# Gate and up projections as Strassen's seven products in three of four feed-forward blocks, with weight sums and residual updates by accumulating DMA

## The chip, the cores and the metric

One core of a Trainium2 chip runs the whole kernel. The metric is the device time of one execution in microseconds. TensorE multiplies, VectorE, ScalarE and Pool (GpSimd) do the elementwise work, SP and Pool issue the DMAs; each engine works through its own instructions in order.

## The reference

Two layers of a transformer block on a latent stream of 512 tokens (A) and a context stream of 256 tokens (C), both 1024 wide. Each layer is a feed-forward block (FFN), four token mixers in parallel with an output projection, and a second FFN. What the change touches is the FFN:

```python
def pre_norm(h, g, shift, scale):
    return rms_norm(h, g) * (1.0 + scale) + shift

def swiglu(h, wg, wu, wd):
    return (jax.nn.silu(h @ wg) * (h @ wu)) @ wd

x = x + 0.5 * mx[2] * swiglu(pre_norm(x, norm1_g[i], mx[0], mx[1]), ffn1_wg[i], ffn1_wu[i], ffn1_wd[i])
```

The hidden width is 2816, that is 22 blocks of 128. `mx` and `mc` are nine modulation vectors per layer, a 1024 x 9216 product of the conditioning vector. In the second layer only stream A is needed after the mixers, so of the four FFNs three run on both streams (768 tokens) and the last on A alone. All of it is in fp32.

## The kernel before

Activations stand transposed, channels on partitions and tokens along the free axis. An fp32 product is made of three matmuls (`mm3`, L286 to L288): every operand is split into a rounded high part and the rest, and high x high, high x low and low x high are added up in PSUM. The normed input is kept as such a pair, `xnh` and `xnl`, for A and for C.

`ffn` runs over the 22 hidden blocks in groups of 6, 6, 5 and 5. For a block, `weight` loads a 128 x 1024 tile for the gate and one for the up projection (`wr`, on SP's queue), ScalarE rounds it to `wh` (L265) and VectorE subtracts to get `wl` (L270). Per tile there are 8 contraction steps of three matmuls for C (256 columns) and for A (512 columns, or two halves A0 and A1 in the first `NS` blocks). ScalarE applies SiLU (L322), VectorE multiplies (L323), and the result is split into `hh` and `hl`. After a group, its down projection runs over 8 output chunks, and VectorE adds each result, times the gate `modG`, to the residual `x` (L344).

The last group's down projection goes in three passes (C, A0, A1), each with its own loads of the down weights. Within it the sum of squares of the new residual is gathered (`sumsq`: square on ScalarE, sum on Pool, or on VectorE for the end of A1), and `norm` (L256 to L260: two operations on VectorE and one on ScalarE per chunk, after a row statistic `nsum`, `rb` that passes TensorE, VectorE and Pool) makes the next stage's input for one part while the next part is still being projected.

The modulation vectors (`ada`, L157 and L160) are computed beside the FFNs: Pool loads 128 x 1024 tiles, `AB` buffers deep, and VectorE reduces each against one or two vectors; `fill` hands them out at an even rate. 128 tiles and 224 reductions are spread over the three two-stream FFNs. PSUM has eight banks in three rings, `p` (4), `r` (2) and `d` (2).

The order of instructions within each engine's queue is not that of the program text: a planner orders them ahead of time by its own estimate of durations, with the program's order as priority; buffers are given out in that order too.

## Time and profile before

| | us |
|---|---|
| median of three runs | 3222.77 |
| lowest, highest | 3219.68, 3239.86 |
| the profiled execution: time | 3218.36 |
| the profiled execution: span from first to last instruction | 3216.6 |

The profile is one execution. Busy time counts an engine's instructions; matmuls overlap in the array, so TensorE's busy share is not its share of the peak. In a timeline a row's duration can reach into the next row's start, so the distance between starts is the pace. The first FFN lies at 46 to 606 us, the second at about 1226 to 1762, the third at 1762 to 2320 and the last at 2838 to 3206.

### The profile page before, as it was taken

The page shows a single profiled execution, that of the slowest core. Times are in us where ns is not written, and L with a number is a line of the kernel's source. Part 1 is how long each engine was busy: PE and PEld are TensorE (multiplying, and loading weights), DVE is VectorE, ACT ScalarE, POOL GpSimd, SP SyncE. Part 2 cuts the span into 40 slices and gives each one's busy share as a digit, 9 for nine tenths or more (in the row PEclk, how much of TensorE's full clock was granted, in tenths as well). Part 3 has the DMA queues.
Part 4 walks back from the last instruction along what each step waited for, and adds up shares of the span by engine and source line. Part 5 has one row for each costly group of instructions (what it writes and reads, how often), then busy time and mean ns, then how long its engine had stood idle before and what let it go on. Part 6 is the DMA issues. An engine that isn't in the chain of part 4 may idle for free.

```text
span 3216.6 us, 48071 instructions
## 1 busy us (share of the span) xinstructions
PE 3092.6 (96%) x19394; PEld 2699.5 (84%) x19394; DVE 1670.6 (52%) x2964; ACT 1061.2 (33%) x1912; POOL 391.3 (12%) x646
## 2 busy tenths in 40 slices
PE   7999999998999999999999999999997899999998
PEld 4888888886788888888889988888885788788887
DVE  4994232736855449994236332323646745353334
ACT  3212112545444433121224212122455353342223
POOL 1110000410233011120002000000311332000001
PEclk9999999998999999999999999999998999899999
DMA  6662221514543335683124221212523523323333
GB/s 246 200 204 59 70 68 48 176 56 125 153 98 89 85 127 180 202 264 120 53 73 125 61 64 60 73 53 68 149 74 121 149 73 83 122 87 99 96 99 105
DMA packets 133485, 358.42 MB, mean 111 GB/s; under 512 B 17968, under 2 KB 31792, under 8 KB 132880
## 3 DMA queue, kind: packets, MB, share of 16 engines
q1 hardware_dynamic: 101200, 256.52, 26.0%
q0 software_dynamic: 32064, 98.85, 10.9%
q8 instruction: 152, 2.49, 0.3%
q14 instruction: 69, 0.57, 0.1%
HBM read 317.94 MB, written 39.65 MB: 111 GB/s over the span
## 4 chain that ended last, share of the span: by engine, by line
PE 55%; DVE 3%; DMA 1%; ACT 1%; issue 1%; POOL 0%; SPq 0%; POOLq 0%; DVEq 0%; ACTq 0%
PE dacc L286 4%; PE dacc L287 4%; PE dacc L288 4%; PE uA L288 4%; PE uA L286 4%; PE uA L287 4%; PE gA L287 4%; PE gA L286 4%; PE gA L288 4%; PE guC L288 3%; PE guC L286 3%; PE guC L287 3%; PE o L738 2%; PE pj L286 1%; PE pj L288 1%; PE pj L287 1%
## 5 line engine op out<-in xcount | busy, mean ns | idle before, releaser
L265 ACT CAST wh<-wr 128x1024 fp32r<-128x1024 f32 (+5 forms) x443 | 394.8, 893 | 1262.9 <-PE dacc L287 452.8
L270 DVE TENSOR_TENSOR wl<-wr,wh 128x1024 fp32r<-128x1024 f32 (+5 forms) x443 | 459.6, 1040 | 411.3 <-ACT wh L265 391.0
L286 PE MATMUL dacc<-hh,wh 128*128 128x256 f32 (+1 forms) x1392 | 451.3, 326 | 1.7 <-ACT wh L265 1.5
L288 PE MATMUL dacc<-hh,wl 128*128 128x256 f32 (+1 forms) x1392 | 450.7, 326 | 1.4 <-DVE wl L270 1.3
L287 PE MATMUL dacc<-hl,wh 128*128 128x256 f32 (+1 forms) x1392 | 452.1, 326 | 0.0
L286 PE MATMUL guC<-xnhC,wh 128*128 128x256 f32 x1056 | 298.8, 284 | 3.3 <-ACT xnhC L259 1.7
L288 PE MATMUL guC<-xnhC,wl 128*128 128x256 f32 x1056 | 299.4, 284 | 0.9 <-DVE wl L270 0.9
L287 PE MATMUL guC<-xnlC,wh 128*128 128x256 f32 x1056 | 299.0, 283 | 0.0
L160 DVE CUSTOM_DVE_ANT_0 adao<-adaw,silr,adab 128x1024 f32<-128x1024 f32 x224 | 287.1, 1282 | 11.8 <-DMA adaw<-ada_t 8.5
L286 PE MATMUL gA<-xnhA,wh 128*128 128x512 f32 (+1 forms) x752 | 284.2, 379 | 2.0 <-ACT xnhA L259 2.0
L286 PEld LDWEIGHTS dacc<-hh,wh 128*128 128x128 f32 x1392 | 261.4, 188 | 27.7 <-ACT wh L265 2.6
L287 PE MATMUL gA<-xnlA,wh 128*128 128x512 f32 (+1 forms) x752 | 282.9, 378 | 1.0 <-DVE xnlA L260 1.0
L288 PEld LDWEIGHTS dacc<-hh,wl 128*128 128x128 f32 x1392 | 261.2, 188 | 26.9 <-DVE wl L270 2.0
L288 PE MATMUL uA<-xnhA,wl 128*128 128x512 f32 (+1 forms) x752 | 283.0, 376 | 0.6 <-DVE wl L270 0.6
L286 PE MATMUL uA<-xnhA,wh 128*128 128x512 f32 (+1 forms) x752 | 283.1, 376 | 0.4 <-ACT wh L265 0.4
L287 PE MATMUL uA<-xnlA,wh 128*128 128x512 f32 (+1 forms) x752 | 283.1, 376 | 0.0
L288 PE MATMUL gA<-xnhA,wl 128*128 128x512 f32 (+1 forms) x752 | 282.8, 376 | 0.0
L287 PEld LDWEIGHTS dacc<-hl,wh 128*128 128x128 f32 x1392 | 261.4, 188 | 25.0
L344 DVE SCALAR_TENSOR_TENSOR xA<-dacc,modG,xA 128x512 f32<-128x512 f32 (+1 forms) x160 | 102.1, 641 | 253.5 <-PE dacc L288 253.2
L286 PEld LDWEIGHTS guC<-xnhC,wh 128*128 128x128 f32 x1056 | 202.3, 192 | 7.4 <-ACT wh L265 2.4
L287 PEld LDWEIGHTS guC<-xnlC,wh 128*128 128x128 f32 x1056 | 202.9, 192 | 2.7
L288 PEld LDWEIGHTS guC<-xnhC,wl 128*128 128x128 f32 x1056 | 203.0, 192 | 1.9 <-DVE wl L270 1.5
(352 smaller groups left out, 5737.7 us busy)
## 6 DMA issues: line engine op xcount, KB each, us to landing
wr<-wgu SPq DMA_DIRECT2D x176, 512.0 KB, 3.6
adaw<-ada_t POOLq DMA_DIRECT2D x128, 512.0 KB, 4.4
wr<-wd SPq DMA_DIRECT2D x120, 320.0 KB, 3.0
wr<-wd SPq DMA_DIRECT2D x64, 384.0 KB, 3.2
wr<-win SPq DMA_DIRECT2D x44, 512.0 KB, 3.7
adaw<-ada_w SPq DMA_DIRECT2D x32, 256.0 KB, 5.2
hl<-eh SPq DMA_DIRECT2D x32, 192.0 KB, 3.1
hl<-el SPq DMA_DIRECT2D x24, 192.0 KB, 3.4
```

Source lines behind the costliest of these rows:

```text
L160: nc.vector.tensor_tensor_reduce(o, w, self.silr[:, v], 1.0, self.adab[:, l, m:m + 1], ALU.mult, ALU.add, self.mods[l][:, m, v:v + 1])
L265: nc.scalar.copy(hi, src)
L270: (nc.vector if leng == "V" else nc.gpsimd).tensor_tensor(lo, src, hi.bitcast(F32), op=ALU.subtract)
L286: nc.tensor.matmul(out, lhsT=wh, rhs=xh, start=start, stop=False)
L287: nc.tensor.matmul(out, lhsT=wh, rhs=xl, start=False, stop=False)
L288: nc.tensor.matmul(out, lhsT=wl, rhs=xh, start=False, stop=stop)
L344: nc.vector.scalar_tensor_tensor(out=x, in0=acc, scalar=gate[:, i, m, r:r + 1], in1=x, op0=ALU.mult, op1=ALU.add)
L738: nc.tensor.matmul(o[:, q0 + q], lhsT=p[:, q * 128:q * 128 + 128], rhs=v(kb), start=False, stop=kb == 3 and q == n // 128 - 1)
```

## The change

In the three two-stream FFNs `ffn` is replaced by `ffn2`. A block's gate and up weights, over the two halves of the 1024 channels, are a 2 x 2 matrix of 128 x 512 tiles (A11, A12 for the gate, A21, A22 for up), and the normed input is a 2 x 2 matrix (two halves of the channels by two halves of 384 tokens, each 256 of A and 128 of C). Winograd's form of Strassen's scheme gives the four results with seven products of 4 contraction steps instead of eight. `sums7` forms the sums of the inputs once per FFN, after block 0, which is computed in the plain way; the fourth of them takes the place of a quarter of the normed input. `chunk7` makes one block: the weight sums S1 and S3 are made by loading one tile and accumulating another onto it by a DMA that Pool issues, S2 and S4 on VectorE; each of the seven sources is split by `block`. Two blocks overlap, seven slots apart, with their products in turn. The results are added on VectorE as they leave PSUM.

The down projection goes in groups of 3 blocks (the last of 4), one output chunk per slot, three slots after a group's last block. Except in the last group, ScalarE evacuates the result times the gate into `y`, and an accumulating DMA from Pool adds `y` to the residual. Weight buffers hold 512 columns, eight raw ones and five pairs of split ones; the modulation has two buffers instead of four, and its scratch output is shared with `sumsq`. Projections of stream A that permute tokens go in two halves of 256 columns. The last FFN keeps `ffn`, for A alone. The scratch for Pool's DMA descriptors is halved. The core of the diff:

```diff
-AB = 4
-NS, LAG = [0, 2, 2, 2], 2
+AB = 2
+LAG = 2
 NR = "r"
 SSV, SSM = ("A1",), 5
+
+RB, BB, WAIT = 8, 5, 3
 PASSES = {1: [["A0"], ["A1"]], 2: [["C"], ["A0"], ["A1"]]}
+
+GROUPS2 = [(f, f + 3) for f in range(0, 18, 3)] + [(18, 22)]
+SLOTS = 7
...
+        self.XN = {w: [p.tile([128, 4, 2, 384], F32R, name="xn%s%d" % (w, i)) for i in range(2)] for w in "hl"}
...
-                    o = self.wa.tile([128, 1024], F32, tag="wo", name="adao", bufs=1)
+                    o = self.fs.tile([128, TX], F32, tag="sq", name="adao", bufs=1).bitcast(BF16)
...
+        if self.wblk:
+            if w <= 512:
+                raw = self.wp.tile([128, 512], F32, tag="wd", name="wd", bufs=2)
+                self.nc.sync.dma_start(out=raw[:, :w], in_=ap)
+                bs = [self.block(raw[:, :w])]
+            else:
+                bs = []
+                for c in range(0, w, 512):
+                    raw = self.wp.tile([128, 512], F32, tag="wr", name="wr", bufs=RB)[:, :min(w - c, 512)]
+                    self.nc.sync.dma_start(out=raw, in_=ap[:, c:min(w, c + 512)])
+                    bs.append(self.block(raw))
+            return Cols([b[0] for b in bs]), Cols([b[1] for b in bs])
...
+    def block(self, src):
+
+        w = src.shape[-1]
+        hi = self.wp.tile([128, 512], F32R, tag="bh", name="wh", bufs=BB)
+        lo = self.wp.tile([128, 512], F32R, tag="bl", name="wl", bufs=BB)
+        self.split(src, hi[:, :w], lo[:, :w])
+        return hi, lo
...
+    def ffn2(self, l, i, save, then):
+        nc = self.nc
+        fi = 0 if i == 0 else 1
+        up, dn, gate = self.I["wgu"], self.I["wd"], self.modG
+        H = {}
+        def hid(f):
+            H[f] = [self.hp.tile([128, 768], F32R, tag=t, name=t).rearrange("p (h t) -> p h t", h=2) for t in ("hh", "hl")]
+            return H[f]
+        W = [self.weight(up[l, fi, 0, :, j], 1024) for j in range(2)]
+        temps = {kk: [self.hp.tile([128, 768], F32, tag=t, name="x" + t).rearrange("p (k c) -> p k c", k=2)
+                      for t in ("hh", "hh", "hl", "hl")] for kk in (0, 2)}
+        hh, hl = hid(0)
+        for u in self.units(["A", "C"]):
+            gu = self.psum((128, 2, TC), name="gu", ring="p")
+            for j in range(2):
+                wh, wl = W[j]
+                for k in range(KD):
+                    self.mm3(self.two(gu[:, j], u), wh[:, k * 128:(k + 1) * 128], wl[:, k * 128:(k + 1) * 128],
+                             self.xn("h", u, k), self.xn("l", u, k), k == 0, k == KD - 1)
+            sg = self.fs.tile([128, 384], F32, tag="sg", name="sg", bufs=1)[:, :TC]
+            h = self.fs.tile([128, 384], F32, tag="s1", name="h")[:, :TC]
+            nc.scalar.activation(sg, gu[:, 0], ACTF.Silu)
+            nc.vector.tensor_tensor(h, sg, gu[:, 1], op=ALU.mult)
+            self.split(self.two(h, u), self.tok(hh, u), self.tok(hl, u))
+        self.sums7(temps)
+        def down(f0, f1, m, us, last):
+            nf = f1 - f0
+            while (l, 3 * i + 2) not in self.adone:
+                self.sided += 1
+                next(self.side)
+            wh, wl = self.weight(dn[l, fi, m, :, f0:f1].rearrange("p f c -> p (f c)"), nf * 128)
+            for v in us:
+                p, cols, t = self.unit(v)
+                r = 0 if p == "A" else 1
+                acc = self.psum((128, t), name="dacc", ring=None if last else "d")
+                if not last and v == us[0]:
+                    y = self.wp.tile([128, TX + TC], F32, tag="y", name="y", bufs=2)
+                for f in range(f0, f1):
+                    c = slice((f - f0) * 128, (f - f0) * 128 + 128)
+                    self.mm3(self.two(acc, v), wh[:, c], wl[:, c], self.tok(H[f][0], v), self.tok(H[f][1], v), f == f0, f == f1 - 1)
+                if not last:
+                    nc.scalar.activation(y[:, 0:TX] if p == "A" else y[:, TX:], acc, ACTF.Copy, scale=gate[:, i, m, r:r + 1])
+                    continue
+                x = self.X[p][:, m, cols]
+                nc.vector.scalar_tensor_tensor(out=x, in0=acc, scalar=gate[:, i, m, r:r + 1], in1=x,
+                                               op0=ALU.mult, op1=ALU.add)
+                self.sumsq(v, m)
+                if p in save:
+                    nc.gpsimd.dma_start(out=self.xd[p][:, m, cols], in_=x)
+            if not last:
+                nc.gpsimd.dma_start(out=self.X[""][:, m], in_=y, accum_op=ALU.add)
+        order = sorted((SLOTS * (f - 1) + 2 * n, f, n) for f in range(1, NF) for n in range(SLOTS))
+        chunks, tasks, gi = {}, [], 0
+        for t, f, n in order:
+            if n == 0:
+                chunks[f] = self.chunk7(up[l, fi, f], hid, f)
+            next(chunks[f], None)
+            if n == SLOTS - 1 and f == GROUPS2[gi][1] - 1 and f < NF - 1:
+                tasks += [(t + WAIT, *GROUPS2[gi], m) for m in range(KD)]
+                gi += 1
+            if tasks and tasks[0][0] <= t:
+                down(*tasks.pop(0)[1:], ("C", "A"), False)
+            self.fill((t + 1) / (SLOTS * (NF - 1)))
+        for k in tasks:
+            down(*k[1:], ("C", "A"), False)
+        due = []
+        for us in PASSES[2]:
+            for m in range(KD):
+                if due and m >= LAG:
+                    then(due.pop(0))
+                down(*GROUPS2[-1], m, us, True)
+            due += us
+        for u in due:
+            then(u)
+    def sums7(self, temps):
+        nc = self.nc
+        self.T7 = {w: [self.tp7.tile([128, 4, 384], F32R, name="t%s%d" % (w, n)) for n in range(3)] for w in "hl"}
+        for c in (slice(256, 384), slice(0, 256)):
+            for kk in (0, 2):
+                ks = slice(kk, kk + 2)
+                x12, x22, x11, x21 = [t[:, :, c] for t in temps[kk]]
+                for x, i, j, e in ((x12, 0, 1, nc.vector), (x22, 1, 1, nc.vector), (x11, 0, 0, nc.gpsimd), (x21, 1, 0, nc.gpsimd)):
+                    e.tensor_tensor(x, *[self.XN[w][i][:, ks, j, c].bitcast(F32) for w in "hl"], op=ALU.add)
+                minus = dict(scalar=-1.0, op0=ALU.mult, op1=ALU.subtract)
+                nc.vector.tensor_tensor(x11, x11, x12, op=ALU.subtract)
+                nc.vector.tensor_tensor(x12, x22, x12, op=ALU.subtract)
+                nc.vector.scalar_tensor_tensor(out=x22, in0=x11, in1=x22, **minus)
+                nc.vector.scalar_tensor_tensor(out=x21, in0=x22, in1=x21, **minus)
+                for x, n in ((x22, 1), (x11, 0), (x12, 2)):
+                    self.split(x, *[self.T7[w][n][:, ks, c] for w in "hl"])
+                self.split(x21, *[self.XN[w][0][:, ks, 1, c] for w in "hl"])
+    def chunk7(self, ap, hid, f):
+        nc = self.nc
+        def raw(j, h, *more):
+            t = self.wp.tile([128, 512], F32, tag="wr", name="wr", bufs=RB)
+            nc.sync.dma_start(out=t, in_=ap[:, j, 512 * h:512 * h + 512])
+            for j, h in more:
+                nc.gpsimd.dma_start(out=t, in_=ap[:, j, 512 * h:512 * h + 512], accum_op=ALU.add)
+            return t
+        S1 = raw(1, 0, (1, 1))
+        A11 = raw(0, 0)
+        S3 = raw(0, 0, (1, 0))
+        A12 = raw(0, 1)
+        A22 = raw(1, 1)
+        T = lambda n: [self.T7[w][n] for w in "hl"]
+        B = lambda i, j: [self.XN[w][i][:, :, j] for w in "hl"]
+        s = lambda: self.wp.tile([128, 512], F32, tag="ws", name="ws", bufs=2)
+        small = lambda tag: self.fs.tile([128, 384], F32, tag=tag, name=tag, bufs=1 if tag in ("u3", "sg") else 2)
+        def product(bank, src, x, first):
+            wh, wl = self.block(src)
+            for k in range(4):
+                c = slice(k * 128, k * 128 + 128)
+                self.mm3(bank, wh[:, c], wl[:, c], x[0][:, k], x[1][:, k], first and k == 0, k == 3, True)
+        add = lambda e, o, a, b, op=ALU.add: e.tensor_tensor(o, a, b, op=op)
+        a = self.psum((128, 384), name="pa", ring="p")
+        product(a, A11, B(0, 0), True)
+        s1 = small("s1")
+        nc.scalar.copy(s1, a)
+        yield
+        b = self.psum((128, 384), name="pb", ring="p")
+        S2 = s()
+        add(nc.vector, S2, S1, A11)
+        product(b, S2, T(1), True)
+        u2 = small("u2")
+        add(nc.vector, u2, b, s1)
+        yield
+        c = self.psum((128, 384), name="pc", ring="r")
+        product(c, S1, T(0), True)
+        S4 = s()
+        add(nc.vector, S4, A12, S2)
+        yield
+        product(b, S3, T(2), False)
+        u3 = small("u3")
+        add(nc.vector, u3, b, s1)
+        add(nc.vector, u3, c, u3)
+        yield
+        product(a, A12, B(1, 0), False)
+        sg = small("sg")
+        nc.scalar.activation(sg, a, ACTF.Silu)
+        yield
+        product(c, S4, B(1, 1), False)
+        add(nc.vector, u2, c, u2)
+        nc.scalar.activation(u2, u2, ACTF.Silu)
+        hh, hl = hid(f)
+        nc.vector.scalar_tensor_tensor(out=u3, in0=u2, scalar=-1.0, in1=u3, op0=ALU.mult, op1=ALU.mult)
+        self.split(u3, hh[:, 1], hl[:, 1])
+        yield
+        product(b, A22, B(0, 1), False)
+        add(nc.vector, s1, b, s1)
+        nc.vector.scalar_tensor_tensor(out=s1, in0=sg, scalar=-1.0, in1=s1, op0=ALU.mult, op1=ALU.mult)
+        self.split(s1, hh[:, 0], hl[:, 0])
...
-            for u in self.units([p], halves):
+            for u in self.units([p], halves or (perm and p == "A")):
...
-        if l == 1:
-            self.beside([])
-        self.ffn(l, 2, parts, (), then, NS[2 * l + 1])
+        if l == 0:
+            self.ffn2(l, 2, (), then)
+        else:
+            self.ffn(l, 2, then, 2)
...
-    nc = bacc.Bacc("TRN2", target_bir_lowering=False, num_devices=1, dynamic_dma_scratch_size=4096)
+    nc = bacc.Bacc("TRN2", target_bir_lowering=False, num_devices=1, dynamic_dma_scratch_size=2048)
```

## Rows read from the trace of the kernel before

**Rows 1.** The page: busy us (share of the span) and instructions of each engine.

```profile
PE 3092.6 (96%) x19394; PEld 2699.5 (84%) x19394; DVE 1670.6 (52%) x2964; ACT 1061.2 (33%) x1912; POOL 391.3 (12%) x646
```

**Rows 2.** Busy time by stretch: stretch, length, then each engine, granted clock, DMA share, GB/s.

```profile
0.00:46.00 46.00, 24.13 (x84) 6.64 (x84) 11.79 (x26) 15.39 (x24) 7.51 (x13) 1.00 0.93 346
46.00:98.00 52.00, 50.84 (x278) 44.74 (x279) 44.88 (x75) 19.35 (x32) 6.64 (x15) 0.93 0.44 144
98.00:554.00 456.00, 456.00 (x2627) 402.01 (x2626) 233.78 (x353) 92.82 (x136) 19.90 (x37) 1.00 0.35 106
...
1706.00:1764.00 58.00, 57.56 (x438) 55.16 (x437) 42.20 (x76) 32.54 (x61) 19.18 (x20) 1.00 0.51 141
1764.00:1816.00 52.00, 51.48 (x385) 49.30 (x384) 26.54 (x51) 18.32 (x34) 0.71 (x1) 1.00 0.26 82
1816.00:2264.00 448.00, 448.00 (x2585) 395.42 (x2585) 133.81 (x183) 91.60 (x134) 0.00 (x0) 1.00 0.21 62
```

**Rows 3.** TensorE's timeline, third FFN: start, us, line, operation, tiles, shape.

```profile
1815.83 0.28 PE L286 MATMUL guC<-xnhC,wh 128*128 128x256 f32 x1
...
1821.46 0.28 PE L288 MATMUL guC<-xnhC,wl 128*128 128x256 f32 x1
1821.58 0.40 PE L286 MATMUL gA<-xnhA,wh 128*128 128x512 f32 x1
...
1831.81 0.39 PE L286 MATMUL uA<-xnhA,wh 128*128 128x512 f32 x1
```

**Rows 4.** VectorE's timeline around the third seam (same columns; idle time in brackets).

```profile
1701.20 0.69 DVE L323 TENSOR_TENSOR h<-sg,uA 128x512 f32<-128x512 f32 x1 [3.38 <-PE uA L288]
1701.81 0.82 DVE L270 TENSOR_TENSOR wl<-wr,wh 128x640 fp32r<-128x640 f32 x1
...
1762.78 0.47 DVE L344 SCALAR_TENSOR_TENSOR xA<-dacc,modG,xA 128x256 f32<-128x256 f32 x1
1763.17 0.41 DVE L222 TENSOR_TENSOR ssA<-ssA,sq 128x256 f32<-128x256 f32 x1
1763.50 0.47 DVE L260 SCALAR_TENSOR_TENSOR xnlA<-nt,mod,xnhA 128x256 fp32r<-128x256 f32 x1
```

**Rows 5.** Groups by line and form, whole span: count, busy us, mean ns, idle before.

```profile
L160 DVE CUSTOM_DVE_ANT_0 adao<-adaw,silr,adab 128x1024 f32<-128x1024 f32 x224 | 287.1, 1282 | 11.8 <-DMA adaw<-ada_t 8.5
...
L157 POOL DMA_DIRECT2D adaw<-ada_t x128 | 68.4, 535 | 353.6 <-DVE mod L160 328.3 <-DVE modG L189 12.2 <-DVE wl L270 11.1
...
L265 ACT CAST hh<-h 128x512 fp32r<-128x512 f32 x88 | 54.7, 622 | 9.4 <-DVE h L323 7.3
...
L222 POOL TENSOR_TENSOR ssA<-ssA,sq 128x256 f32<-128x256 f32 x48 | 42.0, 875 | 472.0 <-issue 345.9 <-DVE ssA L222 89.1 <-ACT sq L221 36.5
```

**Rows 6.** DMA issues: tiles, queue, count, size, median us to landing.

```profile
wr<-wgu SPq DMA_DIRECT2D x176, 512.0 KB, 3.6
adaw<-ada_t POOLq DMA_DIRECT2D x128, 512.0 KB, 4.4
...
ka<-hl POOLq DMA_DIRECT2D x12, 384.0 KB, 4.5
...
qa<-hl POOLq DMA_DIRECT2D x8, 384.0 KB, 6.9
```

**Rows 7.** Waits of SP's DMA queue: us in total, times, longest.

```profile
SPq L278 <- DVE wl L270: 2125.8, 391, 30.6
```

**Rows 8.** The third seam: the last down matmuls (tile view), TensorE's and VectorE's timeline.

```profile
L288 PE MATMUL dacc<-hh,wl x120: 277/280/362, 1717.8 to 1762.4; 128*128 128x256 f32 x120
...
1776.77 0.59 PE L236 MATMUL rb<-dg,ones 128*128 128x256 f32 x2
...
1784.03 0.88 DVE L260 SCALAR_TENSOR_TENSOR xnlA<-nt,mod,xnhA 128x256 fp32r<-128x256 f32 x2 [0.19 <-ACT xnhA L259]
```

**Rows 9.** TensorE's timeline at the first FFN's start.

```profile
51.24 0.63 PE L287 MATMUL gA<-xnlA,wh 128*128 128x512 f32 x1
51.67 0.63 PE L288 MATMUL gA<-xnhA,wl 128*128 128x512 f32 x1
```

More of the change, by code (lines that the diff above doesn't have):

```diff
@@ L328, in ffn @@
             due = []
-            for us in PASSES[len(parts)] if last else [self.units(parts, False)]:
+            for us in PASSES[1] if last else [["A"]]:
                 for m in range(KD):
@@ L1349, in run @@
         self.ada_prep()
+        self.adone = set()
         for l in range(2):
```

163 lines of the change are left out of this document (89 added, 74 removed).

## The prediction

> **What bounds the kernel now.** I read the busy shares first: TensorE is busy for 96% of the span, VectorE for 52% [rows 1]. A share is an average, so the next view is the busy time by stretch [rows 2]. In 98:554 and 1816:2264, the middle of the first and the third feed-forward block (FFN), TensorE is busy for every microsecond, at full granted clock, with VectorE at 51% and 30% (233.78 of 456, 133.81 of 448). There nothing but matmul time counts. At the seams it is different: in 1706:1764 and 1764:1816, where one FFN ends and the next begins, VectorE has 42.20 of 58 and 26.54 of 52 us and TensorE loses about half a microsecond in each. So time can be gained by fewer matmul columns in the middles, and lost where the seams, or VectorE, become the limit.
>
> The pace of a matmul is its start-to-start distance, not its duration. From the first to the last of 48 matmuls of 256 columns there are 47 steps in 5.63 us, 0.1198 us each; of 512 columns, 45 steps in 10.23 us, 0.2273 us each [rows 3]. There is no row with 384 columns. Bounds are those two; 384 lies half way, so I take the middle, 0.1735 us. The mean over all 2585 matmuls of 1816:2264 (half of each kind) is 448/2585 = 0.1733 us [rows 2].
>
> **What is removed.** A block of 128 hidden columns costs today 48 matmuls of 512 and 48 of 256 columns for gate and up: 48 x (0.2273 + 0.1198) = 16.66 us. Seven products are 7 x 4 x 3 = 84 matmuls of 384: 84 x 0.1735 = 14.57 us. The saving is 2.09 us per block, for 21 blocks (block 0 stays plain) in three FFNs: 63 x 2.09 = 131.7 us. The down projection keeps its columns, 24 x 0.3471 = 8.33 us a block, so a block takes 22.9 us instead of 25.0. The fourth FFN is as before. Six projections a layer go from 512 to twice 256 columns, 12 x 24 x 0.012 = 3.5 us; block 0 in thirds costs under 1. I carry +4.
>
> **What is added, in the middles.** VectorE per block: seven low halves and two weight sums of 128x512 at 0.61 us start to start [rows 4] = 5.5; five operations of 384 from PSUM and four from SBUF, between 0.39 (256 from PSUM; 0.33 from SBUF) and 0.61 [rows 4], taken at 0.50, = 4.5; 8/3 low halves of down weights at about 0.5 = 1.3; the modulation, 224 reductions at 1.28 over 66 blocks [rows 5], = 4.4. That is 15.7 of 22.9 us, 69% (16.9 us, 74%, in the first FFN, which has 96 of the 224). ScalarE: seven casts at 0.62 [rows 5], five of 384 at 0.52, 8/3 down casts and 8/3 evacuations of C and A, = 4.3 + 2.6 + 4.0 = 11 us, 48%. Pool: two accumulating loads, 8/3 stores and 1.9 modulation loads at 0.54 [rows 5], 3.6 us. No engine exceeds TensorE. The residual update leaves VectorE for ScalarE and the DMA.
>
> What does a fuller VectorE cost TensorE? The rows give both ends: in the middles nothing; in 1706:1764, at 73%, 0.44 of 58 us (0.8%); in 46:98, at 86% (44.88 of 52), 1.16 us (2.2%) though that includes the start [rows 2]. I take 1.5% of 63 x 22.9 = 1443 us, +21 us, nearest to the 73% row; the ends are 0 and 5%, 72 us (each product now waits for an add and hands its bank on, which no row of before has).
>
> DMA per block: five loads of 256 KB (1.31 MB), two accumulating ones (0.52), down weights (0.52), modulation (1.02), residual stores of 128x768 (8/3 x 0.39 = 1.05): 4.4 MB in 22.9 us, 193 GB/s. 0:46 moved 346 GB/s [rows 2]. If an accumulated byte counts twice it is 6.0 MB, 262 GB/s: still below. Eight weight buffers for five tiles a block put a load some six slots (20 us) ahead of its use, against 3.6 us to landing for a weight load, and on Pool's queue 4.4 us for 512 KB and 4.5 to 6.9 us for 384 KB [rows 6]. SP spends 2125.8 us waiting for buffers [rows 7], so loads are far ahead today. Two modulation buffers instead of four still leave 21 us per buffer for 4.4 us of load. I cost these at nothing; the cover is those 20 us. The thin place is the store: `y` has two buffers, a slot with a down step lasts 2.08 + 3.12 = 5.2 us, so a store must be issued and landed within 2 x 5.2 - 1.6 (evacuation and Pool's issue) = 8.8 us. Its price lies between 4.5 us and twice 6.9; I take 6.9, the slower plain row, which fits. What is late if it doesn't: ScalarE stands at the next evacuation, with the weight casts of the next products queued behind it, and TensorE waits for those.
>
> The Trainium skill ("Collectives: The Full Stack", section "The bandwidth ceiling") speaks against this: an add inside a DMA reads two sources on one ring, and the add collective measured there ran at half the copying one's rate. No run here shows it yet. By it the store would be estimated at up to 2 x 4.5 = 9.0 us, just over the limit.
>
> **What is added, at the seams.** This is the other large term. `sums7` forms three new inputs (and overwrites a fourth) before most products can start. On VectorE it is ten operations for each of two 512-element and two 256-element pieces: 20 x 0.61 + 20 x 0.33 = 19 us. Only the C half can run early; the A half needs the last norm. Take the third seam: the last down matmul starts at 1762.4, the row statistics reach `rb` at 1776.8, the last norm's low half ends at 1784.9 [rows 8]. Today blocks 0 and 1 cover it with their C and A0 parts, 4 x 5.75 = 23 us. Afterwards, from 1784.9: 12.2 us of A sums less the last three splits (1.8), some 4 us of C sums that found no gap, 2 us of block 0's own work: the first product with a sum can finish only near 1801, 39 us after the last down matmul. TensorE has 17.3 us of block 0 and A11's product for blocks 1 and 2 (2 x 2.08 = 4.2): 21.5 us. Nothing more: the sums' scratch takes all four buffers of `hh` and of `hl`, so block 0's hidden values stay in the two buffers of `s1` until half of the sums is done, and bank `a` can't be copied out for A12's product. About 17 us of idleness remain. The final passes have four blocks instead of five: 8 x 12 x 0.12 = 11.5 us of TensorE each, against 8 x (0.39 + 0.61 + 2 x 0.39) = 14.2 us of VectorE where a norm runs beside them; +3 after today's slack. After the idle stretch ahead of 46 us the 512-column pace was 0.43 instead of 0.23 us [rows 9], and the mean clock of 0.93 in 46:98 [rows 2] puts 14% of 52 us, 7 us, at half speed: +2. That is 22 us. The first FFN has no passes ahead of it and already loses 1.16 us and the half-speed stretch: 17. The second follows an output projection whose final norm starts some 10 us sooner behind its last matmul (no passes with a norm beside them): 12. Together 51 us. Ends: 5 a seam (C sums hidden, a good order) and 30 (Pool's four adds at 0.87 us for 256 elements [rows 5] in the way): 15 to 90.
>
> **Sum**, against the profiled execution's own 3218.4 us (span 3216.6 and 1.8 around it): 3218.4 - 131.7 + 4 + 21 + 51 = 3162.7. That execution is 4.4 us below the median of the runs, inside their spread; I forecast 3163 us.
>
> **Rivals.** *A. Everything is covered.* Seams at 5, middles at 0: 3218.4 - 131.7 + 4 + 15 = 3106. For it: TensorE is fully busy in the middles today. Against: the seams' VectorE work is serial behind the last norm. *B. VectorE and ScalarE set the pace of the products.* Each of 63 x 7 = 441 products has a cast, a subtraction and an evacuation on in-order queues, with modulation reductions of 1.28 us between them. At 0.23 us lost per product, 101 us instead of 21: 3243, no change that can be told; at 0.3 us 3274. For it: 69 to 74% load; against: five block buffers put casts some four products ahead. *C. The accumulating store is slow,* and the change ends slower. One mechanism, the `y` round trip: each microsecond of landing beyond 8.8 costs 0.5 us for each of 3 x 48 = 144 down steps, 72 us. The gain of 56 us is gone at 9.6 us, the time is over 1% longer from 10.0 us; at 10.8 us, 3163 + 144 = 3307. For it: no row has such a DMA, and one plain row is at 6.9. Against: 4.5 us is the commoner row for this size, and queues are a third used.
>
> **How the numbers follow.** Forecast, with its own range of 3110 to 3205: 0.47. A: 0.15. B: 0.23. C: 0.15. About 1% (32 us) is what a measurement of this kernel can tell from no change. Faster (below 3190): 0.43 of the forecast's chance, all of A, 0.03 of B: 0.61. Same (3190 to 3255): 0.04, 0.16 of B, 0.02 of C: 0.22. Slower: 0.04 of B, 0.13 of C: 0.17. The range runs from A's side, 3090, to B's upper part, 3260; it leaves out most of C and the edges, 2 in 10.
>
> **What would show it.** Matmuls of 384 columns 0.173 us apart; the middles of the three FFNs about 8% shorter, TensorE over 98% busy with VectorE at 69 to 74%; an idle stretch of 10 to 20 us on TensorE at each FFN's start, released by VectorE's splits of the sums; stores landing in under 8.8 us. Wrong if ScalarE waits at `y` for a DMA (C), if TensorE waits in the middles for `wl` or for an add (B), or if no seam shows an idle stretch (A). A 384-column pace nearer 0.18 would take 34 us from the gain by itself.

## The result: slower by 3%

The changed kernel takes 3325.15 us (median; 3321.50 to 3328.81), the kernel before 3223.88 in the same comparison: a ratio of 1.0305, 95% interval 1.0268 to 1.0342. The forecast was 3163, with a range that ended at 3260.

From the first and last starts of the products in both traces, in us (the spans add up to 3216.6 and 3324.3; in the kernel before the second FFN begins at 1198.7, not at about 1226, and the third at 1760.6):

| stretch | before | after | difference |
|---|---|---|---|
| ahead of the first FFN | 46.4 | 48.8 | +2.4 |
| first FFN | 559.7 | 585.5 | +25.8 |
| mixers and projection, layer 0 | 592.6 | 608.8 | +16.2 |
| second FFN | 561.9 | 589.8 | +27.9 |
| third FFN | 559.4 | 586.7 | +27.3 |
| mixers and projection, layer 1 | 510.3 | 517.0 | +6.7 |
| the rest | 386.3 | 387.7 | +1.4 |

Each changed FFN was to become some 20 us shorter and became 26 to 28 us longer. The page's busy line, against [rows 1]: TensorE has less to do and a smaller share, VectorE 340 us more.

```profile
PE 3072.5 (92%) x18808; PEld 2757.7 (83%) x18808; DVE 2012.2 (61%) x3803; ACT 1397.8 (42%) x2735; POOL 671.5 (20%) x948
```

TensorE's timeline, as in [rows 3], now with 384 columns: four steps in 0.70 us, 0.175 us each (0.1735 was forecast):

```profile
303.39 0.33 PE L350 MATMUL pb<-tl,wh 128*128 128x384 f32 x1
303.56 0.34 PE L351 MATMUL pb<-th,wl 128*128 128x384 f32 x1
...
304.09 0.34 PE L351 MATMUL pb<-th,wl 128*128 128x384 f32 x1
```

The products are nearly as cheap as forecast, so the loss is waiting. Busy time by stretch (columns as in [rows 2]) shows where: the start, the middle in two halves, the tail of the first FFN, and the start of the third:

```profile
48.00:140.00 92.00, 76.32 (x381) 70.46 (x382) 82.94 (x166) 36.78 (x76) 28.10 (x28) 0.81 0.47 116
140.00:380.00 240.00, 221.76 (x1229) 205.27 (x1228) 205.49 (x367) 95.30 (x187) 58.89 (x82) 0.99 0.85 220
380.00:580.00 200.00, 200.00 (x1144) 190.34 (x1143) 104.61 (x181) 93.52 (x176) 33.09 (x38) 1.00 0.63 138
585.00:636.00 51.00, 43.28 (x301) 37.63 (x299) 34.15 (x68) 23.23 (x49) 25.47 (x39) 1.00 0.57 169
1836.00:1930.00 94.00, 67.02 (x344) 60.29 (x344) 89.61 (x165) 31.97 (x66) 25.14 (x31) 0.84 0.52 147
```

From 380 on the middle is what was forecast: TensorE busy all the time, VectorE at 52%. In 140:380 TensorE lacks 18 us and VectorE is busy for 205 of 240. VectorE's mean over both halves is 310 of 440, 70%, the forecast's 69 to 74%; but the planner works the modulations off ahead of 380, and there VectorE has no room at all, since it also stands idle:

```profile
L198 DVE CUSTOM_DVE_ANT_0 adao<-adaw,silr,adab 128x1024 bf16<-128x1024 f32 x224 | 288.8, 1289 | 95.1 <-DMA adaw<-ada_t 94.1
DVE adao L198 <- DMA adaw<-ada_t: 29.7, 18, 2.9
```

The first line is the group of the reductions over the whole span: beside 289 us of work 94 us of idle time ahead of them for late loads, where [rows 5] had 8.5. The second is VectorE's waits in 140:380: 29.7 us of it there. Busy and blocked together are 235 of 240 us. Why loads are late is read from Pool's timeline (start, us; idle time ahead and its releaser in brackets):

```profile
258.73 0.89 POOL L461 DMA_DIRECT2D x<-y  x1 [0.76 <-ACT y L452]
264.26 0.88 POOL L520 DMA_DIRECT2D wr<-wgu  x1 [4.64 <-DMA wr<-wgu]
264.89 0.82 POOL L195 DMA_DIRECT2D adaw<-ada_t  x1
```

The accumulating half of a weight sum waits 4.64 us for its first half to land, and the modulation load stands behind it in Pool's queue. At 270.91 VectorE reaches the reduction of such a load and has been idle for 2.93 us; every split and sum queued behind it is as late.

What TensorE itself waits for in 140:380, some 18 us in all, is mixed (its three largest waits, and one of ScalarE's):

```profile
PE dacc L349 <- ACT y L452: 4.8, 3, 2.6
PE pc L349 <- DVE u L539: 4.4, 2, 2.5
PE pb L349 <- DVE s L539: 3.0, 3, 1.9
...
ACT y L452 <- DMA x<-y: 40.3, 13, 5.7
```

VectorE's adds, which free the PSUM banks, come late; and so does the evacuation into `y`: ScalarE stands 40.3 us there for a residual store that has not landed.

DMA issues, as in [rows 6]: over the whole run the store, for which the forecast wanted under 8.8 us, lands after 5.6; modulation loads take 5.9 instead of 4.4. In 140:380 alone (last line) the store takes 7.1, and 10.7 at most.

```profile
adaw<-ada_t POOLq DMA_DIRECT2D x128, 512.0 KB, 5.9
x<-y POOLq DMA_DIRECT2D x144, 384.0 KB, 5.6
wr<-wgu POOLq DMA_DIRECT2D x126, 256.0 KB, 4.8
...
x<-y POOLq DMA_DIRECT2D x24, 384.0 KB, 7.1
```

### The profile page after: what moved, and what is told of

Its sections match the earlier page's. It is cut to its first block, busy times and chain, and to the rows that moved or that the text cites. A ratio compares the mean times of both kernels' runs of the same rounds, so it can differ in the third digit from the quotient of the medians.

```text
span 3324.3 us, 50373 instructions
## 1 busy us (share of the span) xinstructions
PE 3072.5 (92%) x18808; PEld 2757.7 (83%) x18808; DVE 2012.2 (61%) x3803; ACT 1397.8 (42%) x2735; POOL 671.5 (20%) x948
## 3 DMA queue, kind: packets, MB, share of 16 engines
q1 hardware_dynamic: 144336, 269.90, 27.3%
q0 software_dynamic: 70944, 188.52, 25.8%
## 4 chain that ended last, share of the span: by engine, by line
PE 41%; DVE 8%; DMA 8%; issue 3%; ACT 1%; POOL 0%; DVEq 0%; POOLq 0%; ACTq 0%; SPq 0%
DMA adaw<-ada_t 4%; PE dacc L349 3%; PE dacc L351 3%; PE dacc L350 3%; DVE wl L313 2%; PE pb L351 2%; PE pb L350 2%; PE pb L349 2%; DVE adao L198 2%; PE o L964 2%; DMA wr<-wgu 1%; PE gA L349 1%; PE uA L351 1%; PE pc L351 1%; PE uA L349 1%
## 5 line engine op out<-in xcount | busy, mean ns | idle before, releaser
L308 ACT CAST wh<-wr 128x512 fp32r<-128x512 f32 (+4 forms) x491 | 344.2, 706 | 624.0 <-PE dacc L350 179.2
L313 DVE TENSOR_TENSOR wl<-wr,wh 128x512 fp32r<-128x512 f32 (+4 forms) x491 | 392.2, 802 | 333.9 <-ACT wh L308 321.4
L198 DVE CUSTOM_DVE_ANT_0 adao<-adaw,silr,adab 128x1024 bf16<-128x1024 f32 x224 | 288.8, 1289 | 95.1 <-DMA adaw<-ada_t 94.1
L349 PE MATMUL pj<-xnh,wh 128*128 128x256 f32 (+2 forms) x768 | 252.6, 330 | 17.8 <-ACT wh L308 15.1
L351 PE MATMUL pj<-xnh,wl 128*128 128x256 f32 (+2 forms) x768 | 246.6, 324 | 7.7 <-DVE wl L313 7.7
L350 PE MATMUL pj<-xnl,wh 128*128 128x256 f32 (+2 forms) x768 | 248.1, 324 | 0.0
L452 ACT ACTIVATE y<-dacc,modG 128x256 f32<-128x256 f32 (+1 forms) x288 | 166.6, 580 | 169.6 <-DMA x<-y 107.8
L349 PE MATMUL pb<-th,wh 128*128 128x384 f32 x504 | 172.4, 343 | 16.9 <-DVE s L539 9.4
L350 PE MATMUL pb<-tl,wh 128*128 128x384 f32 x504 | 172.5, 342 | 5.9 <-DVE tl L313 5.9
L349 PE MATMUL pa<-xnh,wh 128*128 128x384 f32 x504 | 171.4, 340 | 4.1 <-ACT wh L308 2.9
L351 PE MATMUL pa<-xnh,wl 128*128 128x384 f32 x504 | 170.9, 340 | 3.7 <-DVE wl L313 3.7
```

The costliest lines, as they stand in the source:

```text
L198: nc.vector.tensor_tensor_reduce(o, w, self.silr[:, v], 1.0, self.adab[:, l, m:m + 1], ALU.mult, ALU.add, self.mods[l][:, m, v:v + 1])
L308: nc.scalar.copy(hi, src)
L313: (nc.vector if leng == "V" else nc.gpsimd).tensor_tensor(lo, src, hi.bitcast(F32), op=ALU.subtract)
L349: nc.tensor.matmul(out, lhsT=wh, rhs=xh, start=start, stop=False, skip_group_check=more)
L350: nc.tensor.matmul(out, lhsT=wh, rhs=xl, start=False, stop=False, skip_group_check=more)
L351: nc.tensor.matmul(out, lhsT=wl, rhs=xh, start=False, stop=stop, skip_group_check=more)
```

## The experiments

All times are medians of compared runs. One caution holds throughout: with every edit the planner orders all queues anew, and may move work between stages, so each is read by stage as well as by its total.

### One part undone at a time

**sq_two** gives the squares of the last passes two buffers:

```diff
+            if self.wblk and t == TC:
+                sq = self.fs.tile([128, 384], F32, tag="s1", name="sq", bufs=2)[:, :t]
...
```

> The changed kernel (3325 us) with one thing undone: the squares of 256 columns for the norms get two buffers again (the idle pair s1) instead of one. Theory TAIL (the single buffer makes ACT's squares and the adding engine take turns, so that the norm behind each FFN and behind the output projection comes some 5 to 10 us late, at five places): 3285 to 3305 us, and the row sum of squares of the first FFN ends within 4 us of the last down product instead of 13 us. Rival theory COVER (what bounds the ends of the FFNs is VectorE's and the weights' work in the last passes, and the squares lie beside it): 3318 to 3328 us.

3297.39 us, 28 less, as theory TAIL had it; the reason holds for part. The two stretches behind FFNs 1 and 3 are 11.3 and 4.6 us shorter. In the changed kernel ScalarE's squares and the adding engine take turns behind the last down product (634.3), from 637.6 to 646.1:

```profile
639.54 0.42 ACT L260 ACTIVATE sq<-x 128x256 f32<-128x256 f32 x1 [1.55 <-POOL ssA L261]
...
644.33 0.42 ACT L260 ACTIVATE sq<-x 128x256 f32<-128x256 f32 x1 [1.57 <-POOL ssA L261]
645.24 0.42 ACT L260 ACTIVATE sq<-x 128x256 f32<-128x256 f32 x1 [0.49 <-DVE ssA L261]
```

But the squares still end 8 us behind the last product, not within 4. The other 12 us go with the planner's order: it moved the third FFN's modulations into the second, where 72 loads now stand in the middle instead of 34. The second FFN took 613.7 us (24 more), the third 543.3 (43 less). That gave the next question.

**wd_ring** loads the last passes' down weights into the eight buffers `wr`:

```diff
+                if last:
+                    raw = self.wp.tile([128, 512], F32, tag="wr", name="wd", bufs=RB)
```

> The changed kernel with one thing changed: in the last passes the down weights are loaded into the eight buffers of the gate and up weights, idle by then, instead of the two buffers wd. Theory RING (with two buffers the load of a down weight is exposed: about 0.6 us in each of 24 steps of 3 tails): the three tails lose 41 us less of TensorE, 3285 to 3300 us. Rival theory DVE (the tails are bound by VectorE's and ACT's splits, evictions and squares, so the loads come earlier and wait): 3315 to 3328 us.

3305.38 us, 20 less and 5 above what theory RING gave. It holds for the tails: in the changed kernel ScalarE waits in 584:636 for the weights' DMA ("ACT wh <- DMA wd", first line), and with the ring TensorE is busy for all of the tail, which is 39 us instead of 51 (second line, busy time in the tail). The three tails are some 42 us shorter, but half is given back: mixers +6 and +8.5, the third FFN's start +14.

```profile
ACT wh L308 <- DMA wd<-wd: 19.4, 15, 3.5
```

```profile
583.00:622.00 39.00, 38.97 (x315) 38.50 (x313) 28.98 (x52) 19.05 (x38) 19.02 (x31) 1.00 0.57 190
```

**resid_dve** takes the residual update back to VectorE; **sums_dve** makes S1 and S3 there from plain loads:

```diff
...
-                if not last:
-                    nc.scalar.activation(y[:, 0:TX] if p == "A" else y[:, TX:], acc, ACTF.Copy, scale=gate[:, i, m, r:r + 1])
-                    continue
...
-            if not last:
-                nc.gpsimd.dma_start(out=self.X[""][:, m], in_=y, accum_op=ALU.add)
```

```diff
-            for j, h in more:
-                nc.gpsimd.dma_start(out=t, in_=ap[:, j, 512 * h:512 * h + 512], accum_op=ALU.add)
...
+        nc.vector.tensor_tensor(S1, S3, A22, op=ALU.add)
+        nc.vector.tensor_tensor(S3, A11, S3, op=ALU.add)
```

> The changed kernel with the residual updates of the middles back on VectorE straight from PSUM (as in the kernel before), without the copy on ACT, its buffers y and the accumulating store. Theory QUEUE (in the middles TensorE waits because the stores, the weight sums and the modulation loads stand in one in-order Pool queue, each behind another engine's work or a landing of 5 to 6 us): the stores gone, the 75 us extra of the middles fall by 20 to 45 us, 3280 to 3305 us, with VectorE at 80 to 84% in the middles. Rival theory LOAD (VectorE's work sets the pace wherever TensorE waits): 144 x 1.0 us more on VectorE cost 20 to 60 us, 3345 to 3385 us.

> The changed kernel with the weight sums S1 and S3 made by VectorE from four plain loads, so that no weight is accumulated by DMA (126 accumulating transfers of 256 KB, and 63 plain ones, are gone). Theory QUEUE: Pool's queue holds only the residual stores and the modulation loads, DMA share of the middles falls from 0.78 to about 0.6, time 3290 to 3310 us. Rival theory LOAD (VectorE sets the pace; 126 x 0.61 us = 77 us more on it): 3330 to 3360 us. That neither matters, since loads and sums are ahead by more than a chunk: 3320 to 3330 us.

3291.67 and 3281.41 us: 34 and 44 less, with 152 and 70 us **more** busy time on VectorE. That VectorE's load by itself sets the pace is refuted; theory QUEUE holds, for the sums by more than it said. VectorE's idle time ahead of reductions with late loads, in 140:560, goes from 29.7 us to 4.7 and 14.4, and TensorE loses 6 and 4 us in 140:380 instead of 18. Each edit takes more than the queue's order away: the DMA engines' share in 140:380 falls from 0.85 to 0.64 and 0.73, and ScalarE's wait for stores there from 40.3 us to nothing (no stores) and 13.1; these two runs do not divide the gain among the three.

### The modulations

**no_mods** leaves them out of the changed kernel, **before_no_mods** out of the kernel before (constants set once; there all three lists of modulations are empty).

```diff
-        self.side, self.sides, self.sided = self.ada(js), 8 * len(js), 0
+        self.side, self.sides, self.sided = iter(()), 8 * len(js), 0
...
```

> The changed kernel without the modulation work beside the feed-forwards: the 128 loads of 512 KB and their 224 to 235 reductions of 1.28 us on VectorE are left out, and constants stand in their place (the first two of layer 0, made ahead of the first norm, stay). Theory FRONT (the middles lose their time while the modulations are worked off, which the schedule does in the first half of each: 140 to 380 us TensorE is busy 34 to 38 of 40 us with VectorE at 31 to 36; from 380 on 40.0 with VectorE at 19 to 23): periods of 22.5 us a block, 60 to 90 us less, 3235 to 3265 us. Rival theory STORE (the in-order Pool queue and the landings of the residual stores set the losses): 10 to 30 us less, 3295 to 3315 us.

> The kernel before, without the modulation work beside the feed-forwards (constants in its place, as in the run no_mods). Leaving it out of the changed kernel saved 114 us. Theory SLACK (VectorE at 50% and blocks of 25 us hid all of it before, so that the change exposed it): 3210 to 3228 us. Rival theory ALWAYS (its loads and reductions cost much the same in both kernels): 3110 to 3160 us.

3211.26 and 3226.13 us. In the changed kernel the modulations cost 114 us, more than the 60 to 90 of theory FRONT; in the kernel before nothing (ratio 1.0004, 0.9992 to 1.0016), as theory SLACK had it. Without them the bad half of the middle has TensorE busy for all of it, in **no_mods**:

```profile
140.00:380.00 240.00, 240.00 (x1377) 228.30 (x1377) 122.66 (x212) 111.71 (x211) 43.55 (x50) 1.00 0.69 150
```

A block then takes 23.1 us (nine blocks from the SiLU at 166.6 to that at 374.4), so products, stores and accumulating sums alone run nearly as forecast (22.9): rival C by itself is out. The store lands there after 5.4 us in 140:380, 7.1 at most, and ScalarE waits 5.9 us for it. Is it the reductions' time or their late loads?

**mods_paced** spreads the loads over the middle, **mods_sp** puts them on SP's queue:

```diff
+                elif self.pace is not None:
+                    nc.gpsimd.tensor_copy(w[:, 0:1], self.pace)
```

```diff
-                nc.gpsimd.dma_start(out=w, in_=self.I["ada_t"][l, m])
+                nc.sync.dma_start(out=w, in_=self.I["ada_t"][l, m])
```

> The changed kernel with each modulation load bound to the block of hidden rows just finished (Pool first copies one element a partition from it into the load's buffer), so that the reductions spread over the whole middle, as the program's text has them, instead of its first half. Theory FRONT: VectorE near 70% all through the middles, TensorE 97% or more, periods of 22.9 to 23.3 us, 20 to 45 us less: 3280 to 3305 us. Rival theory SUM (the losses are proportional to the modulations wherever they stand, as they delay VectorE's other work by a fixed time each): 3318 to 3330 us; the copies' waits hold Pool's stores up: above 3330.

> The changed kernel with one thing changed: the modulation loads are issued by SP's queue instead of Pool's, so that they no longer stand behind the residual stores and the weight sums. Theory QUEUE (VectorE stands at a reduction whose load is late, and the splits and sums behind it come late): its idle time for these loads in the first middle falls from 30 us to under 5, and 40 to 80 us of the 114 come back, 3245 to 3285 us. Theory BUSY (the reductions' own 2.56 us a load are what costs): 3315 to 3330 us. That the loads on SP hold the weights' loads up: above 3330 us.

3358.21 us, 33 more: theory FRONT, that an even spread is enough, is refuted for this queue, and the time is that of the last clause (stores held up by the copies' waits). The rows of mods_paced say what counts: in 140:380 VectorE is busy for only 155 of 240 us, and TensorE has lost more than before, 25 us; in 140:600 VectorE stands 94.3 us at reductions whose loads are late, since Pool's queue now waits at the copies too (45.2 us).

```profile
140.00:380.00 240.00, 215.35 (x1175) 200.05 (x1174) 154.64 (x272) 92.73 (x179) 53.91 (x81) 0.96 0.72 171
```

```profile
DVE adao L200 <- DMA adaw<-ada_t: 94.3, 22, 9.1
```

mods_sp takes 3298.33 us, 27 less, between the two theories: VectorE's idle time for late loads in the first middle is halved, 14.8 us, not gone. TensorE loses 8 us in 140:380 instead of 18, with the DMA engines as busy as in the changed kernel (0.87 and 0.85), so it is the queue's order that counts here and not the traffic alone:

```profile
140.00:380.00 240.00, 232.20 (x1289) 219.44 (x1288) 209.78 (x376) 104.68 (x201) 38.39 (x44) 0.97 0.87 226
```

Nor is it the two buffers by themselves: with Pool's queue to themselves (four_undone, below) the loads leave no such idle time with the same two. So the queue is part of the 114 us; that VectorE's own 289 us, in stretches where it is full anyway, are the rest is likely and not shown.

**no_sums** prices the starts: the tables T are filled with a constant and `sums7` ends there.

```diff
+                nc.gpsimd.memset(t.bitcast(F32), 0.5)
+        return
```

> The changed kernel without the sums of the normed rows at the start of each feed-forward: the three tables T are filled with a constant by Pool, and the fourth sum, which takes the place of a quarter of the rows, is left out too. Theory SEAM (these sums, behind the last norm on VectorE, are what holds the first blocks up: the three starts lose 108 us, 15 before): 60 to 90 us less, 3235 to 3265 us. Rival theory REST (norms, modulations behind a late load and the half clock after them make the loss): 5 to 30 us less, 3295 to 3320 us.

3262.35 us, 63 less: theory SEAM. The first SiLU of a product comes 36 to 44 us into an FFN, instead of 50 to 55.

### Parts together

**four_undone** joins sq_two, wd_ring, resid_dve and sums_dve. **five_paced** adds the pacing and a third modulation buffer, in the room that `y` leaves.

```diff
-AB = 2
+AB = 3
```

> The changed kernel with the four edits measured so far together: squares in two buffers, last passes' down weights in the eight buffers, residual updates on VectorE, weight sums on VectorE. Each alone gave 28, 20, 34 and 44 us less. If the four are separate losses: 126 less, 3195 to 3210 us, below the kernel before. If the two moves to VectorE fight for it in the first half of the middles, where it is at 85 to 90%: 3215 to 3245 us.

> The four edits, the modulations paced by the blocks, and a third buffer for the modulation loads in the room that the store's buffers leave. By theory FRONT 15 to 35 us under the kernel with four edits, 3165 to 3190 us; by theory SUM no different from it, within 8 us.

3229.45 and 3232.80 us. The four are not separate: 96 us instead of 126; the pacing changes nothing, as theory SUM had it. Pool's queue now holds modulation loads alone in the middles. VectorE's idle time for them in 140:380 is 0 in four_undone and 10.0 us in five_paced, and the middle is nearly whole in both: with reductions in front, then evenly spread,

```profile
140.00:380.00 240.00, 235.81 (x1329) 222.01 (x1329) 235.73 (x428) 79.22 (x148) 19.36 (x36) 0.99 0.48 143
```

```profile
140.00:380.00 240.00, 236.29 (x1331) 223.79 (x1330) 213.17 (x383) 80.11 (x150) 21.06 (x46) 0.99 0.39 117
```

VectorE busy for 98% or 89%: TensorE loses 4 us either way (18 in the changed kernel). So 98% of work costs less here than 86% of work and 12% of standing blocked in the changed kernel, where stores and accumulating sums share the queue.

**three_undone_sp** keeps the residual store, with modulation loads on SP. **two_plain** is four_undone with a second plain block.

```diff
-        order = sorted((SLOTS * (f - 1) + 2 * n, f, n) for f in range(1, NF) for n in range(SLOTS))
+        order = sorted((SLOTS * (f - 2) + 2 * n, f, n) for f in range(2, NF) for n in range(SLOTS))
```

> The changed kernel with squares in two buffers, last passes' weights in eight, weight sums on VectorE, and the modulation loads on SP's queue; the residual stores by accumulating DMA stay, alone on Pool's queue. Against four_undone (3229 us) VectorE has 151 us less to do. If VectorE's load is what is left: periods of 22.6 to 23.0 us, 3180 to 3210 us. If the store's round trip or SP's queue takes its place: 3230 to 3260 us.

> The kernel with four edits undone (3229 us), with two blocks by plain products ahead of the seven, so that the sums lie beside 33 us of TensorE's work instead of 17; it costs 3 x 2.1 us of products. Theory COVER (TensorE waits at the starts for sums that come behind the norm): the three starts lose 8 to 12 us less each, 3200 to 3218 us. Rival theory BOUND (VectorE is 93 to 100% busy from the norm to some 60 us behind it, so that what the sums no longer delay the rest delays): 3225 to 3240 us.

3230.08 us: store or VectorE makes no difference once the queue is free, and the 3180 to 3210 us for VectorE's load do not come about. two_plain takes 3245.93, 17 more, of which 6 are its products, and 6 above what theory BOUND gave: a longer cover doesn't help. VectorE is busy for 83 to 93% of the first 70 us of its three FFNs, and all the time in 90:150; the first SiLU of a product comes 59 to 63 us into an FFN instead of 50.

**mods_pool** has Pool multiply and ScalarE add up; **mods_sums_pool** gives Pool S1 and S3 too.

```diff
-                    nc.vector.tensor_tensor_reduce(o, w, self.silr[:, v], 1.0, self.adab[:, l, m:m + 1],
-                                                   ALU.mult, ALU.add, self.mods[l][:, m, v:v + 1])
+                    nc.gpsimd.tensor_tensor(o, w, self.silr[:, v], op=ALU.mult)
+                    nc.scalar.activation(o, o, ACTF.Copy, accum_out=self.mods[l][:, m, v:v + 1])
```

> The kernel with four edits undone (3229 us), and the modulation products taken off VectorE: Pool multiplies a loaded row block by the conditioning vector (two of 1024 columns a load, some 3.5 us each by its 0.875 us for 256), ACT adds up along the row. Theory PROPORTION (each pair of reductions, 2.6 us on VectorE, delays what the products wait for, wherever it stands): periods of 22.5 us instead of 23.4, 3150 to 3190 us, under the kernel before. Rival theory LATE (Pool's products slow VectorE or come too late for the gates, or what is lost is the loads' and not the reductions'): 3225 us or more.

> As mods_pool, with the weight sums S1 and S3 on Pool too instead of VectorE (126 of 512 columns, some 1.75 us each by its 0.875 us for 256). If VectorE is still what TensorE waits for, 10 to 25 us less than mods_pool; if Pool's row of work comes to be late for the products, 20 us or more above it.

3376.36 and 3410.52 us, 147 and 181 more than four_undone. Pool's products slow VectorE; whether that is all of the 147 us was not tried. Groups of VectorE in 140:560, in four_undone and then in mods_pool (count, busy us, mean ns):

```profile
L316 DVE TENSOR_TENSOR wl<-wr,wh 128x512 fp32r<-128x512 f32 x89 | 60.8, 683 | 3.1 <-ACT wh L311 3.1
L533 DVE TENSOR_TENSOR u<-pc,u 128x384 f32<-128x384 f32 x38 | 20.9, 550 | 2.8 <-PE pc L357 2.6
```

```profile
L319 DVE TENSOR_TENSOR wl<-wr,wh 128x512 fp32r<-128x512 f32 x76 | 102.2, 1347 | 3.2 <-ACT wh L314 3.1
L536 DVE TENSOR_TENSOR u<-pc,u 128x384 f32<-128x384 f32 x32 | 17.5, 545 | 0.7 <-PE pc L360 0.7
```

A subtraction with both inputs in SBUF takes twice as long beside Pool's products; one that reads PSUM is untouched.

**four_saves_sp** and **three_saves_sp** add two edits, on either base: the saves of `x` go to SP's queue, and the first modulation loads of an FFN wait for the starts' sums.

```diff
-                    nc.gpsimd.dma_start(out=self.xd[p][:, m, cols], in_=x)
+                    nc.sync.dma_start(out=self.xd[p][:, m, cols], in_=x)
...
-                    nc.gpsimd.tensor_copy(w[:, 0:1], self.xn("l", "A1", KD - 1)[:, 0:1].bitcast(F32))
+                    nc.gpsimd.tensor_copy(w[:, 0:1], self.T7["l"][2][:, 3, 255:256].bitcast(F32))
```

> four_undone (3229 us) with two more edits: the saves of x for the second half (24 stores behind each of two FFNs) go on SP's queue instead of Pool's, ahead of whose square sums they stood; and the first modulation loads of each FFN are bound to the last of the starts' sums, so that no reduction stands among norms and sums. Theory SEAM (norms held up in Pool's queue and VectorE full at the starts are what is left): the first norm behind FFN 1 and 3 comes 10 to 18 us sooner and the starts lose 5 to 10 us less, 3180 to 3205 us, under the kernel before. Rival theory WORK (VectorE has the same work to do and is full from the start on, so the reductions only move to where they cost the same; the norm is late for ACT's squares): 3220 to 3235 us.

> three_undone_sp (3230 us) with the same two edits: here the residual stores stay on Pool's queue ahead of the square sums, and modulation loads, weights' loads and saves are all on SP's. By theory SEAM 3180 to 3210 us; by theory WORK 3220 to 3235 us; that a save waiting for VectorE on SP's queue holds the down weights behind it up: above 3235 us.

3220.39 us (ratio 0.9987, 0.9977 to 0.9997) and 3229.33. In four_undone the sums of squares of the first rows stood among the saves in Pool's queue, so that the row statistic of the first norm behind FFN 1 came at 605.4, after all passes; now it comes at 585.4, and the stretch behind FFN 1 is 11 us shorter. This is the best version here, 105 us under the changed kernel and level with the kernel before: its three FFNs are together 24 us shorter than before, its two mixer stretches 22 us longer. Only 9 us are new against four_undone, so of theory SEAM the norm came as said and the time did not: 3220 is the lower edge of what theory WORK gave.

**four_saves_no_mods** leaves the modulations out of that one.

> four_saves_sp (3220 us) without the modulation work (constants in its place, as in no_mods and before_no_mods; the kernel before loses nothing by it). Theory LOAD (after the four edits and the saves VectorE's load is what is left; without the 229 reductions, 293 us, the products' gain shows): periods of 22.5 us, 3140 to 3170 us, 2 to 2.5% under the kernel before. Rival theory ORDER (VectorE only queues at the starts, where norm, sums and splits follow one another, and the middles cost little): 3195 to 3215 us.

3175.45 us, 45 less (ratio to the kernel before 0.9857, 0.9838 to 0.9875), nearer to theory LOAD, whose range it misses by 5 us. The middle of four_saves_sp, then of this one:

```profile
140.00:380.00 240.00, 232.26 (x1298) 217.50 (x1297) 235.99 (x428) 78.28 (x147) 18.85 (x35) 0.99 0.49 144
```

```profile
140.00:380.00 240.00, 240.00 (x1373) 227.86 (x1373) 166.46 (x291) 80.40 (x149) 0.00 (x0) 1.00 0.26 68
```

With VectorE at 69%, the forecast's figure, the seven products give the FFNs 20 to 26 us each (the first 536.6 instead of 559.7); at 98%, in four_saves_sp, they give 5 to 10.

## Why the prediction was wrong

- **The removed matmul time was nearly right.** 0.173 to 0.176 us a matmul; blocks of 23.1 us where nothing else intervenes, 22.9 forecast, and 25.05 before (six blocks in 150.3 us), 25.0 forecast. Some 123 of the 131.7 us were there to be had.
- **The middles' term, 21 us, was the first to fail.** The distances between starts exceed the matmuls' forecast pace by 91 us in the three middles, about 15 before: 76, of which some 8 are the pace itself. The step that failed is the sentence that two modulation buffers leave 21 us for 4.4 us of load and that Pool's queue costs nothing. It counted the landing and Pool's busy time (3.6 us a block), not what an in-order queue does to an instruction behind another's wait. The weight sum waits for its first half, the store for ScalarE, and the load behind them is late; VectorE blocks at it. mods_sp shows this chain with the traffic unchanged; resid_dve, sums_dve and mods_paced agree. The second error was the mean: 69 to 74% was right on average and wrong in each half, 86% (98% with the blocked time) and 52%. That views by stretch matter was the prediction's own first paragraph; the new work was not placed by stretch.
- **The seams' term, 51 us, covered the starts only, and by half.** Starts lose 108 us (15 before), 93 more. The order (sums behind the last norm, VectorE serial) was right: no_sums gives back 63. Not counted were reductions among norms and sums, one of them with 5.33 us of wait for its load at 99.65: without the modulations (no_mods) the first 92 us of the three FFNs lose only 69 us, 56 more than before, close to the forecast's 51. The clock's +2 us a seam were too few as well: the granted clock is 0.81 in 48:140 and 0.84 in 1836:1930, where the kernel before has 0.96 in 46:138 and 1.00 in 1764:1858. In 102:110, after TensorE had stood 3.87 us for VectorE, it is 0.50, the lower of its two levels (1.2 of 2.4 GHz), and matmuls of 384 columns start 0.32 us apart instead of 0.175. How much of the 108 us is clock and how much waiting is not divided.
- **The tails cost 42 us, where +3 had been put for a seam.** The two buffers `wd` and the single `sq` stood in the diff; the prediction priced VectorE's work there and not the round trip of two weight buffers through load, rounding and subtraction. wd_ring shows it.
- **The mixers lost 23 us instead of 4.** The late norms behind the FFNs, from `sq` and from saves ahead of square sums in Pool's queue, are a large part (sq_two gives 16 us back, moving the saves 11 in layer 0, against four_undone); the projections' halves alone were counted. It does not end there: in four_saves_sp, with all of this undone, the two stretches still take 5 and 17 us more than before. The first projection starts 8 to 10 us behind the last down product there, behind shorter tails, and 4 to 5 before; the rest stays open.
- **The rivals.** B, with 3243 to 3274, had the right wait, TensorE waiting for VectorE's adds and splits, but put it on load. C, the store's round trip, came about in part: its sign, ScalarE waiting at `y` for a DMA, shows with 40.3 us in 140:380 and 107.8 in the whole run, and 4.8 of the 18 us that TensorE loses in 140:380 end with ScalarE's evacuation. But it takes the modulations beside it (no_mods: 5.9 us, and TensorE loses nothing), and the landing of 7.1 us there is under the limit of 8.8 in the median. The store's queue mattered more, through those behind it. Taken together: 76 - 21, 93 + 42 - 51, 23 - 4 and some 4 us at the ends: 55 + 84 + 19 + 4 = 162 us, what lies between 3163 and 3325.

By stretch, 72 of the 114 us of the modulations lie in the middles, where TensorE loses 74 us in the changed kernel and 2 in no_mods, and 37 in the first 92 us of the FFNs (106 and 69; measured against the distances between starts at full pace). What stays open is how they divide between late loads and VectorE's own time (mods_sp moves 27 of them). Of the some 30 us by which each FFN of four_saves_no_mods still exceeds its products, 22 to 28 lie in its first 92 us, where VectorE is busy for 81 of 91 us (49:140). That an even spread would be enough on a free Pool queue with the store kept was not tried.

## What to carry to other kernels

When work is moved to an in-order DMA queue, list what each instruction there waits for and who stands behind it: a load queued behind an accumulation that awaits its first half is late, and the engine that consumes it blocks with all its other work. Place the load of every engine by stretch, not by stage, and ask where the planner puts the optional work. Fewer matmuls pay where the elementwise engines have room: here the products gave 20 to 26 us an FFN with VectorE at 69% in the middle, 5 to 10 at 98%.

## What had not been expected of the hardware

- VectorE's `wl` subtraction of 512 columns takes 683 ns, and 1347 ns while Pool multiplies 1024 columns (2.54 us each); with one operand in PSUM, 550 and 545 ns. The Trainium skill ("SBUF — State Buffer", section "Who interferes with whom") says that a VectorE instruction with two SBUF inputs contends with a Pool instruction that reads SBUF, one with a single SBUF input does not: the rows agree.
- An accumulating DMA costs its issuer 0.88 us (256 KB) to 0.95 us (384 KB), where a plain one of 512 KB took 0.535 in [rows 5] and 0.627 in the changed kernel. On Pool's queue 98.85 MB took 10.9% of the DMA engines before and 188.52 MB 25.8% after: by shares times spans, each added MB took some 1.6 times as long as one before; how much of that is the add and how much the mean packet, 2.7 KB instead of 3.1, is not divided. The Trainium skill ("Collectives: The Full Stack", section "The bandwidth ceiling") has an add inside a DMA at half the rate of a copy: these rows lie between, and the store landed in 5.6 us over the whole run and 7.1 in 140:380, not in the 9.0 that had been estimated from it.
